# A gated decoder block: turning K on VectorE instead of TensorE in the second pass, with K times values moved ahead

## The chip, the core and the metric

The kernel runs on one core of a Trainium2 chip. The metric is the device time of one execution in microseconds (us). The kernel before took 1733.4 us, the median of 3 runs (1732.51 to 1734.95).

The engines are named as in the profile: PE (TensorE, matrix products), PEld (its weight loads), DVE (VectorE), ACT (ScalarE), POOL (GpSimd) and SP (SyncE, which only issues transfers). Each engine works off its own instructions strictly in their order and waits where an operand isn't ready.

## The reference, cut to what matters

One layer on 2048 tokens of width 1024. A normalised and modulated input is projected at once into eight parts; one branch is a pooling mixer, the other a gated linear recurrence with 8 heads of 128 channels; both are gated, merged and projected out. The change concerns the recurrence alone. Per head, with f the forget gate, k = 1 - f, and chunks of tokens:

```
o_inter = q * exp(cum) @ state
scores[t, s] = sum_k q[t, k] * k[s, k] * exp(cum[t, k] - cum[s, k])     (s <= t)
o = o_inter + scores @ v
state = exp(last) * state + (k * exp(last - cum)).T @ v
```

The last line, the update of the state, needs K with its decay to the chunk's end, multiplied by the values v with the sum over tokens. TensorE sums over partitions, so tokens have to lie on partitions there. K is made with channels on partitions: it has to be turned.

## The kernel before, in words

The 2048 tokens are done in two passes of 1024 tokens (p = 0 and 1), and each pass in two halves of 512 (t = 0 and 1, tiles of 128 channels x 512 tokens, or four blocks of 128 tokens). A pass goes through the heads 0 to 7. For each head it runs three "quads" of projections. A quad computes a 2x2 block of products by seven products named B11, T1, T2, B21, T3, B22 and T4, in this order, each of 12 matmuls of 128x512. Quad "fq" makes forget gate and query of the head, "m" the merge gates, "gp" a pooling part and the head's output gate (heads 0 to 6 run fq, m, gp; head 7 runs fq, gp, m). A quad accumulates in three PSUM banks: pa (B11, then T2, T3 and T4 on top), pe (T1, then B22) and pb. After T3, DVE adds pa into the tile c22 (L651), after B22 pe into c12 (L655). T4 accumulates into the bank pa that c22's addition reads, so it can't start before that.

Between the products the generator `hgrn` (L677) does the recurrence of the heads, one step per product. The `yield`s in it mark the steps, and both halves t step side by side. The recurrence of a head starts after its fq quad and goes on into the next head's fq and m quads. Its parts, with the names in the profile:

- F, the forget gate, is bounded from below by DVE (L681); Q (sq in the profile) is multiplied by F; a tree of products of F over 2, 4, ... 128 tokens is made in TT (L696).
- The scores are made in four sets, for token distances 1 to 4, to 8 and 16, to 32, and 64, as small matmuls into the bank psa (L756, L805 to L808), five steps apart (GAP, L800). Behind each of the first three, DVE copies the results under masks into PT (L727, L733) and multiplies K by decays one level up (`kup`, L710 to L712), and Q likewise. x32 and x64 are Q with decays for the fourth set.
- With the fourth scores issued, `kup(32)` and `kup(64)` bring K to its last level (L812, L813). These are the DVE rows K<-K,TT of 256 elements.
- Two steps later TensorE turns K by matmuls with the identity into PSUM tile pk (L819), and ScalarE copies that into KS (L821).
- Two steps later again come the products pd = KS x values (L826), four per half, and on DVE the chain SC of states, one block after the other (L831).
- Three steps later follows the output po (L839, L840), with its norm, a turn back (pot) and the gate.

In the second pass the matmuls are held in the order in which the code issues them (`line`, L346 to L353). The other engines' orders come from the framework's scheduler, which also chooses the buffers; so what stands where on DVE is read from the program's order.

Of the kernel before, what the change touches and what calls it, by code (L numbers as in the profile page):

```python
# [8 lines left out]
F32 = mybir.dt.float32  # L9
# [9 lines left out]
P = 128  # L19
SEQ = 2048  # L20
D = 1024
T = 512
NT = T // P
# [3 lines left out]
NH = 8  # L27
# [8 lines left out]
GAP = 5  # L36
# [36 lines left out]
def tile_block(ctx: ExitStack, tc: tile.TileContext, x, w_ada, b_ada, g_post, w_in, pool_w, w_pool_o, w_hgrn_o,  # L73
               w_out, ident_d, mask_d, icnt_d, w_pv_t, x_t, w_quad, w_po, rows_d, out):
    nc = tc.nc
    V, A, G, PE, SP = nc.vector, nc.scalar, nc.gpsimd, nc.tensor, nc.sync
# [14 lines left out]
    px = ctx.enter_context(tc.tile_pool(name="px", bufs=2, space=bass.MemoryType.PSUM))  # L91

    def utile(name, dt=F32):
        return up.tile([P, T], dt, tag="u", name=name)
# [4 lines left out]
    def after(ins):  # L99
        return tc.issue_after(ins.ins) if ins is not None else nullcontext()  # L100
# [245 lines left out]
    def mm(o, l, r, start, stop):  # L346
        with after(line["it"] if line["on"] else None):
            line["it"] = PE.matmul(o, lhsT=l, rhs=r, start=start, stop=stop, skip_group_check=True)  # L348
        return line["it"]

    def turn(o, i):
        with after(line["it"] if line["on"] else None):
            line["it"] = PE.transpose(o, i, ident)  # L353

    def three(ps, w, rhs, start, stop):

        hi, lo = w
        n = len(rhs)
        for k in range(n):
            wh, wl = hi[:, k * P:(k + 1) * P], lo[:, k * P:(k + 1) * P]  # L360
            rh, rl = rhs[k]
            mm(ps, wh, rh, start and k == 0, False)
            mm(ps, wh, rl, False, False)
            mm(ps, wl, rh, False, stop and k == n - 1)
# [126 lines left out]
    def v2(ap, n):  # L491
        return ap.rearrange("p (a b) -> p a b", b=n)

    def bc(ap, n):
        return ap.unsqueeze(2).broadcast_to([P, ap.shape[1], n])

    def tt(o, a, b, op=MUL, e=None):
        return (e or V).tensor_tensor(o, a, b, op=op)  # L498
# [91 lines left out]
    def h_in(p, t, k, cx):  # L590

        if (t, k) in cx["h32"]:
            src = cx["h32"][t, k]
            if t in cx["rr"]:
                tt(src, src, cx["rr"][t])
        else:
            src = px.tile([P, T], F32, tag="px", name=f"xT{p}_{t}_{k}")
            for tk in range(NT):
                xs = cx["xc"][t, k // 2][tk // 2][:, tk % 2, (k % 2) * P:(k % 2 + 1) * P]
                PE.transpose(src[:, tk * P:(tk + 1) * P], xs, ident)  # L600
            cx["h32"][t, k] = utile(f"h32_{p}_{t}_{k}")
        h32 = cx["h32"][t, k]
        A.activation(h32, src, AF.Identity, bias=shv[:, k:k + 1], scale=scv[:, k:k + 1])
        nm = ("B11", "B21", "B12", "B22")[2 * t + k % 2]
        return part(p, nm, k // 2, h32, cx)
# [19 lines left out]
    def quad(name, cx, got, tick):  # L625
# [3 lines left out]
        def prod(ps, nm, start):  # L629
            three(ps, take(), [mv[nm, i] for i in range(4)], start, True)  # L630
# [45 lines left out]

    def hgrn(p, h, t, cx):  # L677
        n = f"{p}_{h}_{t}"
        F, Q = cx["F"].pop((h, t)), cx["Q"].pop((h, t))
        A.activation(F, F, AF.Identity, bias=lb[:, h:h + 1], scale=oml[:, h:h + 1])  # L680
        V.tensor_scalar(F, F, 1e-30, None, op0=MAX)  # L681
# [2 lines left out]
        K = utile("K" + n)  # L684
# [5 lines left out]
        o = 0  # L690
        for hh in (1, 2, 4, 8, 16, 32, 64):
            w = T // (2 * hh)
            a = v2(Tb[hh], 2)
# [10 lines left out]
        def te(hh, i):  # L704
            return v2(Tb[hh], 2)[:, :, i]

        def vv(cc):
            return vh[:, t * NT + cc, :]

        def kup(hh):  # L710
            a = v2(K, 2 * hh)[:, :, 0:hh]
            tt(a, a, bc(te(hh, 1), hh))  # L712

        def qup(hh):
            a = v2(Q, 2 * hh)[:, :, hh:2 * hh]
            tt(a, a, bc(te(hh, 0), hh))
# [3 lines left out]
        def put(dst, src):  # L720

            w = src.shape[2]
            if len(dst.shape) == 3:
                m = mask[:, moff[0]:moff[0] + 4 * w].rearrange("p (a b) -> p a b", b=w)
                moff[0] += 4 * w
                shp = [P, NT, 4, w]
                V.copy_predicated(dst.rearrange("p (c a) b -> p c a b", c=NT), m.unsqueeze(1).broadcast_to(shp),  # L727
                                  src.unsqueeze(2).broadcast_to(shp))
                return
            a, b = dst.shape[2:]  # L730
            m = mask[:, moff[0]:moff[0] + NB * w].rearrange("p (c q a b) -> p c q a b", c=NT, q=4, b=b)
            moff[0] += NB * w
            V.copy_predicated(dst.rearrange("p (c q) a b -> p c q a b", c=NT), m,  # L733
                              src.rearrange("p c (a b) -> p c a b", b=b).unsqueeze(2)
                              .broadcast_to([P, NT, 4, a, b]))

        def blk(ap, b, hh):

            r = ap.rearrange("p (b a w) -> p b a w", b=b, w=2 * hh)[:, :, :, hh:2 * hh]
            return r[:, :, 0, :] if T // b == 2 * hh else r  # L740
# [12 lines left out]
        def scores(X):  # L753
            for i in range(NB):
                r0 = (i % 4) * 32
                mm(s48[r0:r0 + 32, i // 4, 0:48], K[:, i * 32:(i + 1) * 32], X[:, i, :], True, True)  # L756

        def build(hh, b, w):
            X = qp.tile([P, b, 3 * w], F32, tag="qr", name=f"X{hh}_{n}")
            A.copy(sub(X, 0, w, hh), blk(Q, b, hh))  # L760
            qup(hh)
            qo = blk(Q, b, 2 * hh)
            A.copy(sub(X, 1, w, 2 * hh), qo)
            tq = Tb[hh].rearrange("p (a b) -> p a b", b=4)
            xr = sub(X, 2, w, 2 * hh)
            tt(xr, qo, bcb(tq[:, :, 1], b, 2 * hh))
            tt(qo, xr, bcb(tq[:, :, 0], b, 2 * hh))
            return X
# [13 lines left out]
        for hh in (2, 8):  # L782
            scores(X)
            put(blk(ptf, NB, hh), s48[:, :, 0:16])
            put(blk(ptf, NB, 2 * hh), s48[:, :, 16:32])
            put(blk(ptf, NB, 2 * hh), s48[:, :, 32:48])
            kup(hh)
            kup(2 * hh)
            if hh == 2:
                X = build(8, NB, 16)  # L790
            else:
                X = qp.tile([P, T], F32, tag="qr", name=f"X32_{n}")
                x32 = X[:, 0:T // 2].rearrange("p (b w) -> p b w", w=32)
                A.copy(x32, blk(Q, NB // 2, 32))
                qup(32)
                x64 = X[:, T // 2:T].rearrange("p (b w) -> p b w", w=64)
                tq = Tb[32].rearrange("p (a b) -> p a b", b=4)
                q64 = blk(Q, NT, 64)
                tt(x64, q64, bc(tq[:, :, 1], 64))
            for _ in range(GAP):  # L800
                yield
        s64 = s48
        for cc in range(NT):
            o = cc * P
# [4 lines left out]
        A.copy(pt[0:64, :, 64:128], s64[0:64, :, 32:96])  # L809
        A.copy(pt[0:32, :, 32:64], s64[0:32, :, 0:32])  # L810
        A.copy(pt[64:96, :, 96:128], s64[64:96, :, 0:32])
        kup(32)  # L812
        kup(64)  # L813
        tt(q64, x64, bc(tq[:, :, 0], 64))
        yield
        yield
        pk = px.tile([P, T], F32, tag="px", name="pk" + n)
        for cc in range(NT):
            turn(pk[:, cc * P:(cc + 1) * P], K[:, cc * P:(cc + 1) * P])  # L819
        KS = utile("KS" + n)  # L820
        A.copy(KS, pk)  # L821
        yield
        yield
        pd = px.tile([P, NT, P], F32, tag="px", name="pd" + n)
        for cc in range(NT):
            mm(pd[:, cc, :], KS[:, cc * P:(cc + 1) * P], vv(cc), True, True)  # L826
        SC = utile("SC" + n)
# [3 lines left out]
            V.scalar_tensor_tensor(nxt, sts[-1], Tb[128][:, cc:cc + 1], pd[:, cc, :], op0=MUL, op1=ADD)  # L831
            sts.append(nxt)
        carry[h] = sts[NT]
        yield
        yield
        yield
        po = px.tile([P, NT, P], F32, tag="px", name="po" + n)
        for cc in range(NT):
            mm(po[:, cc, :], pt[:, cc, :], vv(cc), True, False)  # L839
# [221 lines left out]
    def a_job(p, j, cx):  # L1061
        w = take()
        sm = sig_in(p, j, 0, cx)
        for t in range(2):
            ps = bank(f"psA{p}_{j}_{t}")
            three(ps, w, [cx["gP"][g, t] for g in range(NG)], True, True)
            tt(sm[t], ps, sm[t])
            cx["a"][j, t] = sm[t]
            tick()
# [300 lines left out]
    for p in range(NPASS):  # L1370
# [3 lines left out]
        if p == 0:  # L1374
# [14 lines left out]
            late = [lambda k=k: h_in(0, 1, k, cxs[0]) for k in range(KT)]  # L1389
# [48 lines left out]
        for h in range(NH):  # L1438
            if 0 < h < NH - 1:
                v_head(p, h + 1, cx)  # L1440
            n = f"{p}_{h}"
# [20 lines left out]
            if h == 0:  # L1462
                for z in range(2):
                    v_head(p, z, cx)
            active.extend(hgrn(p, h, t, cx) for t in range(2))
            if wt:
                pv_merge(h // 2, wt)
# [54 lines left out]
        late = []  # L1522
# [75 lines left out]
```

## Time and profile before

| | us |
|---|---|
| runs, median (lowest to highest) | 1733.4 (1732.51 to 1734.95) |
| the profiled execution | 1732.42 |
| its span in the profile | 1730.6 |
| PE busy | 1706.8 |
| DVE busy | 1223.3 |
| ACT busy | 853.2 |

The profile is of one execution. The heads of the second pass lie at about 1000 to 1500 us. A row of a timeline has the start in us from the span's start, the duration, the engine, the source line, the operation, out<-in and the count of instructions merged; brackets hold the idle time before it and who ended it. A row of a group has, behind the bar, busy us and the mean ns of one instruction, then the idle time before. A row of a table by stage has the stretch, its length, and the busy time of PE, PEld, DVE, ACT and POOL with instruction counts, then TensorE's granted clock, the share of the DMA engines and GB/s.

### The profile page before, as it was taken

The page shows a single profiled execution, that of the slowest core. Times are in us where ns is not written, and L with a number is a line of the kernel's source. Part 1 is how long each engine was busy: PE and PEld are TensorE (multiplying, and loading weights), DVE is VectorE, ACT ScalarE, POOL GpSimd, SP SyncE. Part 2 cuts the span into 40 slices and gives each one's busy share as a digit, 9 for nine tenths or more (in the row PEclk, how much of TensorE's full clock was granted, in tenths as well). Part 3 has the DMA queues.
Part 4 walks back from the last instruction along what each step waited for, and adds up shares of the span by engine and source line. Part 5 has one row for each costly group of instructions (what it writes and reads, how often), then busy time and mean ns, then how long its engine had stood idle before and what let it go on. Part 6 is the DMA issues. An engine that isn't in the chain of part 4 may idle for free.

```text
span 1730.6 us, 31715 instructions
## 1 busy us (share of the span) xinstructions
PE 1706.8 (99%) x11805; PEld 1405.1 (81%) x11805; DVE 1223.3 (71%) x2546; ACT 853.2 (49%) x1951; POOL 96.5 (6%) x151
## 2 busy tenths in 40 slices
PE   7999999999999999999999999999999999999998
PEld 4788888888888887878888888888888888888886
DVE  4668888897988889788787254455455545776666
ACT  5746656566565665342755334344343343434243
POOL 1100000000000000100030000000000000000002
PEclk9999999999999999999999999999999999999999
DMA  9759888788789788976795765665655655565657
GB/s 331 259 185 323 287 303 287 286 300 314 268 293 329 262 289 286 350 252 223 267 313 179 249 208 179 205 202 176 214 193 173 220 180 194 184 226 168 212 197 265
DMA packets 191262, 425.33 MB, mean 246 GB/s; under 512 B 19282, under 2 KB 44546, under 8 KB 191108
## 3 DMA queue, kind: packets, MB, share of 16 engines
q1 hardware_dynamic: 181748, 406.46, 69.2%
q10 hardware_dynamic: 9360, 16.85, 2.6%
q8 instruction: 93, 1.52, 0.4%
q14 instruction: 61, 0.50, 0.1%
HBM read 267.51 MB, written 155.71 MB: 245 GB/s over the span
## 4 chain that ended last, share of the span: by engine, by line
PE 91%; DVE 4%; DMA 2%; ACT 2%; issue 1%; SPq 0%; POOL 0%; DVEq 0%; ACTq 0%; POOLq 0%
PE pafq L348 10%; PE pagp L348 10%; PE pam L348 9%; PE psA L348 5%; PE pegp L348 5%; PE pefq L348 5%; PE pem L348 5%; PE psV L348 4%; PE raB L348 4%; PE psa L348 4%; PE ray L348 3%; PE pbfq L348 3%; PE po L348 2%; PE pbgp L348 2%; PE pbm L348 2%; PE raV L348 2%
## 5 line engine op out<-in xcount | busy, mean ns | idle before, releaser
L193 DVE TENSOR_TENSOR whl<-wr,whl 128x512 fp32r<-128x512 f32 x160 | 109.4, 689 | 38.1 <-ACT whl L192 31.2
L192 ACT CAST whl<-wr 128x512 fp32r<-128x512 f32 x160 | 99.5, 625 | 69.6 <-issue 18.0
L348 PE MATMUL pam<-hT,whl 128*128 128x512 f32 x384 | 128.2, 394 | 0.6 <-ACT c12m L634 0.5
L348 PE MATMUL pagp<-hT,whl 128*128 128x512 f32 x384 | 128.1, 394 | 0.4 <-ACT c12gp L634 0.4
L348 PE MATMUL pafq<-hT,whl 128*128 128x512 f32 x384 | 126.3, 390 | 0.0
L192 ACT CAST whl<-wri 128x512 fp32r<-128x512 f32 x76 | 47.1, 622 | 118.4 <-PE psA L348 31.5
L733 DVE COPY_PREDICATED PT<-mask,psa 128x256 f32<-128x256 uint8 x160 | 86.1, 547 | 11.9 <-PE psa L348 11.9
L348 PEld LDWEIGHTS pagp<-hT,whl 128*128 128x128 f32 x384 | 72.1, 188 | 16.3 <-ACT c12gp L634 0.5
L348 PEld LDWEIGHTS pam<-hT,whl 128*128 128x128 f32 x384 | 72.1, 188 | 15.8 <-ACT c12m L634 1.1
L348 PEld LDWEIGHTS pafq<-hT,whl 128*128 128x128 f32 x384 | 72.1, 188 | 15.2 <-ACT c12fq L634 0.2
L348 PE MATMUL psA<-Ph,whl 128*128 128x512 f32 x256 | 82.5, 395 | 0.6 <-ACT Ph L179 0.6
L348 PE MATMUL psV<-whl,hB 128*128 128x512 f32 x256 | 79.6, 394 | 1.2 <-ACT hB L1330 1.1
L498 DVE TENSOR_TENSOR K<-K,TT 128x256 f32<-128x256 f32 x192 | 80.4, 423 | 0.0
L348 PE MATMUL pagp<-lT,whl 128*128 128x512 f32 x192 | 74.9, 390 | 0.0
L348 PE MATMUL pam<-lT,whl 128*128 128x512 f32 x192 | 74.8, 390 | 0.0
L348 PE MATMUL pafq<-lT,whl 128*128 128x512 f32 x192 | 74.7, 389 | 0.0
L193 DVE TENSOR_TENSOR whl<-wri,whl 128x512 fp32r<-128x512 f32 x76 | 51.8, 686 | 23.8 <-ACT whl L192 23.0
L727 DVE COPY_PREDICATED PT<-mask,psa 128x256 f32<-128x256 uint8 (+1 forms) x96 | 52.0, 542 | 21.7 <-PE psa L348 21.7
L348 PEld LDWEIGHTS psa<-X,K 128*32 128x32 f32 x2816 | 48.6, 110 | 19.8 <-issue 17.5
L861 DVE SCALAR_TENSOR_TENSOR sgg<-pot,vec,sgg 128x512 f32<-128x512 f32 x32 | 23.1, 746 | 54.5 <-PE pot L353 54.5
L681 DVE TENSOR_SCALAR F<-F 128x512 f32<-128x512 f32 x16 | 6.8, 426 | 77.5 <-ACT F L680 77.4
L348 PEld LDWEIGHTS psV<-whl,hB 128*128 128x128 f32 x256 | 47.5, 188 | 14.0 <-ACT hB L1330 1.4
(568 smaller groups left out, 4786.7 us busy)
## 6 DMA issues: line engine op xcount, KB each, us to landing
wr<-in_w_quad_dram SPq DMA_DIRECT2D x88, 256.0 KB, 4.1
whl<-scr_y SPq DMA_DIRECT2D x36, 512.0 KB, 4.7
sm<-Sd SPq DMA_DIRECT2D x64, 256.0 KB, 5.3
whl<-scr_b SPq DMA_DIRECT2D x32, 512.0 KB, 4.0
scr_y<-rfy SPq DMA_DIRECT2D x40, 256.0 KB, 2.9
x<-in_x_dram SPq DMA_DIRECT2D x32, 256.0 KB, 4.8
wa<-in_w_ada_dram SPq DMA_DIRECT2D x32, 256.0 KB, 6.0
V<-Vd SPq DMA_DIRECT2D x16, 512.0 KB, 5.1
```

Of the source, the lines that this page charges most:

```text
L192: A.copy(w[:, 0:T], raw)
L193: V.tensor_tensor(w[:, T:2 * T], raw, w[:, 0:T].bitcast(F32), op=SUB)
L348: line["it"] = PE.matmul(o, lhsT=l, rhs=r, start=start, stop=stop, skip_group_check=True)
L498: return (e or V).tensor_tensor(o, a, b, op=op)
L681: V.tensor_scalar(F, F, 1e-30, None, op0=MAX)
L727: V.copy_predicated(dst.rearrange("p (c a) b -> p c a b", c=NT), m.unsqueeze(1).broadcast_to(shp), src.unsqueeze(2).broadcast_to(shp))
L733: V.copy_predicated(dst.rearrange("p (c q) a b -> p c q a b", c=NT), m, src.rearrange("p c (a b) -> p c a b", b=b).unsqueeze(2) .broadcast ...
L861: V.scalar_tensor_tensor(og, pot, col("ng"), og, op0=MUL, op1=MUL)
```

## The change

In the heads 0 to 6 of the second pass (`by_dve`) TensorE doesn't turn K any more.

- After the third scores, DVE also makes KD: K's first three quarters (blocks of 32 tokens) of each 128 tokens with the decays of `kup(32)` and `kup(64)`. The fourth quarter needs none, and K itself stays as it is. This takes three products per half: one of 256 elements and two of 128.
- In the four steps after that, DVE turns K by 32x32 blocks into KS: `block_turn` j takes the 32 tokens j of all four blocks, and in four instructions, one for each 32 channels, writes 32 partitions of KS from 32 partitions of KD (or K, for j = 3).
- `kup(32)`, `kup(64)`, the turn into pk and ScalarE's copy into KS go.
- pd comes right behind the fourth scores in odd heads, and two steps later in even heads (`late`), where it was four steps later before. The steps behind it are padded so that po stays where it was.

The diff, cut to its core:

```
+    def block_turn(dst, src, j):
+        d, s_ = (a.rearrange("p (c n) -> p c n", n=P) for a in (dst, src))
+        for i in range(4):
+            V.transpose(d[32 * j:32 * j + 32, :, 32 * i:32 * i + 32], s_[32 * i:32 * i + 32, :, 32 * j:32 * j + 32])
...
+        by_dve, late = p > 0 and h < NH - 1, 2 * (h % 2 == 0)
...
-            for _ in range(GAP):
+                if by_dve:
+                    KD, KS = utile("KD" + n), utile("KS" + n)
+                    tt(v2(KD, 64)[:, :, 0:32], v2(K, 64)[:, :, 0:32], bc(te(32, 1), 32))
+                    for o in (0, 32):
+                        tt(v2(KD, P)[:, :, o:o + 32], v2((KD, K)[o // 32], P)[:, :, o:o + 32], bc(te(64, 1), 32))
+            for j in range(GAP):
+                if by_dve and hh == 8 and j:
+                    block_turn(KS, K if j == 4 else KD, j - 1)
                 yield
...
-        kup(32)
-        kup(64)
+        if not by_dve:
+            kup(32)
+            kup(64)
         tt(q64, x64, bc(tq[:, :, 0], 64))
-        yield
-        yield
-        pk = px.tile([P, T], F32, tag="px", name="pk" + n)
-        for cc in range(NT):
-            turn(pk[:, cc * P:(cc + 1) * P], K[:, cc * P:(cc + 1) * P])
-        KS = utile("KS" + n)
-        A.copy(KS, pk)
-        yield
-        yield
+        if by_dve:
+            for _ in range(late):
+                yield
+        else:
...
-        yield
-        yield
-        yield
+        for _ in range(7 - late if by_dve else 3):
+            yield
```

What stands in a row changes at three places. On PE, behind T4 of head 3's fq quad (pafq1_3), where the recurrence of head 2 is at work (1_2 is pass 1, head 2), stood before:

```order
L348 MATMUL pafq1_3_12864<-hT41_3_10758,whl361_12914 128x512
L348 MATMUL pafq1_3_12864<-lT41_3_10759,whl361_12914 128x512
L348 MATMUL pafq1_3_12864<-hT41_3_10758,whl361_12914 128x512
L353 MATMUL pk1_2_0_13025<-ident_87,K1_2_0_12342 128x128 x4
L353 MATMUL pk1_2_1_13032<-ident_87,K1_2_1_12349 128x128 x4
L348 MATMUL pam1_3_13053<-hB111_0_9793,whl362_12930 128x512
```

And at the same place now:

```order
L348 MATMUL pafq1_3_12930<-hT41_3_10758,whl361_12996 128x512
L348 MATMUL pafq1_3_12930<-lT41_3_10759,whl361_12996 128x512
L348 MATMUL pafq1_3_12930<-hT41_3_10758,whl361_12996 128x512
L348 MATMUL pd1_2_0_13111<-V1_2_11488,KS1_2_0_12886 128x128 x4
L348 MATMUL pd1_2_1_13121<-V1_2_11488,KS1_2_1_12916 128x128 x4
L348 MATMUL pam1_3_13145<-hB111_0_9793,whl362_13020 128x512
```

The products pd, which stood two products later, have taken the place of the turn. For odd heads, PE in head 4's fq quad between T3 and B22, in the fourth scores of head 3 (psa1_0 is the half t = 0, psa1_1 the half t = 1):

```order
L348 MATMUL psa1_0_10909<-X32_1_3_0_13596,K1_3_0_13135 32x32
L348 MATMUL psa1_0_10909<-X32_1_3_0_13596,K1_3_0_13135 32x64
L348 MATMUL pd1_3_0_13773<-V1_3_12203,KS1_3_0_13601 128x128 x4
L348 MATMUL psa1_1_10910<-X32_1_3_1_13626,K1_3_1_13142 32x32
L348 MATMUL psa1_1_10910<-sq1_3_1_13035,K1_3_1_13142 32x64
```

Before, the scores of both halves stood together there with no pd among them; now each half's pd follows its scores. On DVE, the end of the work behind head 3's third scores and the beginning of head 4, before:

```order
L498 TENSOR_TENSOR K1_3_1_13050<-K1_3_1_13050,TT1_3_1_13115 128x16x16
L727 COPY_PREDICATED PT1_135<-mask_91,psa1_1_10910 128x16x16
L681 TENSOR_SCALAR F1_4_0_13619<-F1_4_0_13619 128x512
L498 TENSOR_TENSOR c22fq1_4_13587<-pafq1_4_13555,c22fq1_4_13587 128x512
L498 TENSOR_TENSOR sq1_3_0_13022<-X32_1_3_0_13524,TT1_3_0_13107 128x4x64
L498 TENSOR_TENSOR K1_3_0_13043<-K1_3_0_13043,TT1_3_0_13107 128x8x32
```

And now (x4 are the four instructions of one `block_turn`):

```order
L503 TENSOR_TENSOR KD1_3_1_13630<-KD1_3_1_13630,TT1_3_1_13187 128x4x32
L358 STREAM_TRANSPOSE KS1_3_0_13601<-KD1_3_0_13600 32x4x32 x4
L358 STREAM_TRANSPOSE KS1_3_1_13631<-KD1_3_1_13630 32x4x32 x4
L358 STREAM_TRANSPOSE KS1_3_0_13601<-KD1_3_0_13600 32x4x32 x4
L358 STREAM_TRANSPOSE KS1_3_1_13631<-KD1_3_1_13630 32x4x32 x4
L358 STREAM_TRANSPOSE KS1_3_0_13601<-KD1_3_0_13600 32x4x32 x4
L358 STREAM_TRANSPOSE KS1_3_1_13631<-KD1_3_1_13630 32x4x32 x4
L358 STREAM_TRANSPOSE KS1_3_0_13601<-K1_3_0_13135 32x4x32 x4
L358 STREAM_TRANSPOSE KS1_3_1_13631<-K1_3_1_13142 32x4x32 x4
L687 TENSOR_SCALAR F1_4_0_13725<-F1_4_0_13725 128x512
L503 TENSOR_TENSOR c22fq1_4_13677<-pafq1_4_13645,c22fq1_4_13677 128x512
```

The 32 turns of both halves stand in one run, ahead of the next head's F and c22fq, although the code spreads them over four steps: nothing else is left to do on DVE in those steps. The lines of the kernel have moved by 5 there (L681 is now L687, and so on).

More of the change, by code (lines that the diff above doesn't have):

```diff
@@ L811, in hgrn @@
         A.copy(pt[64:96, :, 96:128], s64[64:96, :, 0:32])
-        kup(32)
-        kup(64)
+        if not by_dve:
+            kup(32)
+            kup(64)
         tt(q64, x64, bc(tq[:, :, 0], 64))
-        yield
-        yield
-        pk = px.tile([P, T], F32, tag="px", name="pk" + n)
-        for cc in range(NT):
-            turn(pk[:, cc * P:(cc + 1) * P], K[:, cc * P:(cc + 1) * P])
-        KS = utile("KS" + n)
-        A.copy(KS, pk)
-        yield
-        yield
+        if by_dve:
[3 more added lines that the diff above has]
+            yield
+            yield
+            pk = px.tile([P, T], F32, tag="px", name="pk" + n)
+            for cc in range(NT):
+                turn(pk[:, cc * P:(cc + 1) * P], K[:, cc * P:(cc + 1) * P])
+            KS = utile("KS" + n)
+            A.copy(KS, pk)
+            yield
+            yield
         pd = px.tile([P, NT, P], F32, tag="px", name="pd" + n)
@@ L833, in hgrn @@
         carry[h] = sts[NT]
-        yield
-        yield
-        yield
+        for _ in range(7 - late if by_dve else 3):
+            yield
         po = px.tile([P, NT, P], F32, tag="px", name="po" + n)
```

## The prediction

> **What bounds the kernel now.** I read the page first: its first part, for which engine is full, and its fourth, for which engine the end hangs on.
>
> ```profile
> PE 1706.8 (99%) x11805; PEld 1405.1 (81%) x11805; DVE 1223.3 (71%) x2546; ACT 853.2 (49%) x1951; POOL 96.5 (6%) x151
> PE 91%; DVE 4%; DMA 2%; ACT 2%; issue 1%; SPq 0%; POOL 0%; DVEq 0%; ACTq 0%; POOLq 0%
> ```
>
> TensorE is busy for 99% of the span and carries 91% of the chain. Then the busy time by stage, for two stretches in the heads of the second pass, where the change lies:
>
> ```profile
> 1200.00:1300.00 100.00, 100.00 (x850) 84.06 (x849) 54.39 (x145) 39.81 (x110) 4.81 (x8) 1.00 0.64 203
> 1300.00:1400.00 100.00, 100.00 (x828) 83.19 (x827) 54.28 (x129) 38.43 (x95) 2.40 (x4) 1.00 0.60 192
> ```
>
> The second number is TensorE: it never pauses. VectorE (fourth) is busy just over half the time. So here each microsecond taken off TensorE is a microsecond off the end, each one that TensorE has to wait is one on it, and VectorE work is free as long as it fits between the things TensorE waits for. The average doesn't say whether it fits; the place does.
>
> **What TensorE is spared.** TensorE's timeline from the last fq product of head 1 (pafq) on, with head 0's pk and pd (x8 and x16 are both halves of the sequence):
>
> ```profile
> 1050.92 0.39 PE L348 MATMUL pafq<-hT,whl 128*128 128x512 f32 x1
> ...
> 1053.42 0.39 PE L348 MATMUL pafq<-hT,whl 128*128 128x512 f32 x1
> 1053.65 1.03 PE L353 MATMUL pk<-ident,K 128*128 128x128 f32 x8
> 1054.44 0.48 PE L348 MATMUL pam<-hB,whl 128*128 128x512 f32 x1
> 1054.75 0.40 PE L348 MATMUL pam<-lB,whl 128*128 128x512 f32 x1
> 1054.99 0.62 PE L348 MATMUL pam<-hB,whl 128*128 128x512 f32 x2
> ...
> 1059.75 0.39 PE L348 MATMUL pem<-hT,whl 128*128 128x512 f32 x1
> 1059.98 1.95 PE L348 MATMUL pd<-V,KS 128*128 128x128 f32 x16
> 1061.68 0.48 PE L348 MATMUL pam<-hT,whl 128*128 128x512 f32 x1
> 1061.99 0.40 PE L348 MATMUL pam<-lT,whl 128*128 128x512 f32 x1
> 1062.23 0.62 PE L348 MATMUL pam<-hT,whl 128*128 128x512 f32 x2
> ```
>
> The durations overlap, so the price is taken from starts. Inside a product they lie (1053.42 - 1050.92) / 11 = 0.227 us apart. Three such steps would take 0.68 us; across pk, 1053.42 to 1054.99, they took 1.57. So pk costs TensorE 0.89 us a head, of which 0.79 until the next product starts and 0.10 more in its slow first steps. The same reckoning for pd gives 2.48 - 0.68 = 1.80 us, of which 0.10 is again slow restart.
>
> In the seven heads pk goes: 7 x 0.89 = 6.23 us. In heads 0, 2, 4 and 6 pd takes over pk's place after T4, at its old price. In heads 1, 3 and 5 it goes between the two sequence halves' fourth scores, which already pay the restart, so 3 x 0.10 = 0.30 us goes too. **Gross gain 6.5 us.** ScalarE loses the copy into KS, which is no gain: it isn't on the path. No DMA is moved, and the rows of SP and POOL stand in their old order.
>
> **What VectorE gets, and where.** For each head: six KD products, less the four products K<-K,TT after the next head's c22fq, and 32 turns of 32x4x32. The order shows all 32 in one train, behind the KD products and ahead of the next head's F and c22fq. Between them VectorE waits today; head 3 first, with the last mask copy before the gap:
>
> ```profile
> 1243.45 0.42 DVE L498 TENSOR_TENSOR K<-K,TT 128x256 f32<-128x256 f32 x1
> 1243.78 0.42 DVE L727 COPY_PREDICATED PT<-mask,psa 128x256 f32<-128x256 uint8 x1
> 1253.01 0.43 DVE L681 TENSOR_SCALAR F<-F 128x512 f32<-128x512 f32 x1 [8.80 <-ACT F L680]
> 1254.19 0.69 DVE L498 TENSOR_TENSOR c22fq<-pafq,c22fq 128x512 f32<-128x512 f32 x1 [0.75 <-PE pafq L348]
> ```
>
> And the same F of the heads after 0, 1, 2, 4, 5 and 6:
>
> ```profile
> 1045.42 0.43 DVE L681 TENSOR_SCALAR F<-F 128x512 f32<-128x512 f32 x1 [7.96 <-ACT F L680]
> 1114.64 0.43 DVE L681 TENSOR_SCALAR F<-F 128x512 f32<-128x512 f32 x1 [8.80 <-ACT F L680]
> 1183.76 0.43 DVE L681 TENSOR_SCALAR F<-F 128x512 f32<-128x512 f32 x1 [7.17 <-ACT F L680]
> 1322.14 0.43 DVE L681 TENSOR_SCALAR F<-F 128x512 f32<-128x512 f32 x1 [6.56 <-ACT F L680]
> 1391.38 0.43 DVE L681 TENSOR_SCALAR F<-F 128x512 f32<-128x512 f32 x1 [8.80 <-ACT F L680]
> 1460.51 0.43 DVE L681 TENSOR_SCALAR F<-F 128x512 f32<-128x512 f32 x1 [5.96 <-ACT F L680]
> ```
>
> The gap is 8.80 us after each odd head, and shrinks to 5.96 over the even ones. What a VectorE instruction costs, by starts and by durations:
>
> ```profile
> 1199.82 1.56 DVE L831 SCALAR_TENSOR_TENSOR SC<-SC,TT,pd 128x128 f32<-128x128 f32 x4
> ...
> 1201.90 0.28 DVE L498 TENSOR_TENSOR TT<-TT 128x128 f32<-128x128 f32 x1
> 1202.10 0.34 DVE L831 SCALAR_TENSOR_TENSOR SC<-SC,TT,pd 128x128 f32<-128x128 f32 x1
> ```
>
> ```profile
> L831 DVE SCALAR_TENSOR_TENSOR SC<-SC,TT,pd 128x128 f32<-128x128 f32 x42 | 14.5, 345 | 1.2
> L498 DVE TENSOR_TENSOR TT<-TT 128x128 f32<-128x128 f32 x12 | 3.4, 285 | 0.0
> ```
>
> With 256 elements starts lie 0.33 us apart (1243.45 to 1243.78), with 128 0.20 (1201.90 to 1202.10): neighbours overlap. KD is one of 256 and two of 128 per half: 2 x (0.33 + 0.20 + 0.20) = 1.47 us. So a train starts 1.47 us after the gap opens: in head 3 at 1253.01 - 8.80 + 1.47 = 1245.68.
>
> Of a turn the trace of before shows nothing. It has 128 elements in each of 32 partitions, as many as the TT row. Call X the time from one turn to the next. Low end: 0.20 us, if turns overlap as other instructions do. High end: 0.40 us, the step of the SC chain, each waiting for the one before: (1.56 - 0.345) / 3. Between them lies 0.285, the TT row's whole duration, for turns that neither overlap nor wait for a semaphore. I take **X = 0.31**: nearest that row, plus a little because each turn reads and writes other partitions than its neighbour.
>
> [...]
>
> **Who waits for the train.** Scores of head 3, the B22 product behind them, and the start of T4 after heads 2, 4 and 6 (after head 0 it is the 1050.92 shown above):
>
> ```profile
> 1254.08 0.22 PE L348 MATMUL psa<-X,K 128*32 128x32 f32 x1
> ...
> 1255.60 0.50 PE L348 MATMUL pefq<-hB,whl 128*128 128x512 f32 x1
> ```
>
> ```profile
> 1189.26 0.39 PE L348 MATMUL pafq<-hT,whl 128*128 128x512 f32 x1
> 1327.64 0.39 PE L348 MATMUL pafq<-hT,whl 128*128 128x512 f32 x1
> 1466.01 0.39 PE L348 MATMUL pafq<-hT,whl 128*128 128x512 f32 x1
> ```
>
> Odd heads: the first pd comes after half of the scores, at 1254.08 + 0.76 = 1254.84, and needs turn 28 (its half's last). Fits if 28 X < 1254.84 - 1245.68 = 9.16, X < 0.327. The second pd, a pd half (0.85) and 0.76 later, needs turn 32 and is looser (0.337). Heads 1 and 5 have the same distances.
>
> Even heads: pd is far off, but F and c22fq are queued behind the train, and T4 may not overwrite pafq before c22fq has read it. F and c22fq take about 0.35 + 0.69, with the signal 1.1 us. So 32 X must be under T4's start, less 1.1, less the train's start: in head 0, 1050.92 - 1.1 - 1038.93 = 10.89, X < 0.340; in head 2 10.10, 0.316; in head 4 9.49, 0.297; in head 6 8.89, 0.278.
>
> With X = 0.31: heads 0 to 3 and 5 lose nothing, head 4 waits 9.92 - 9.49 = 0.4 us, head 6 1.0. Net 6.5 - 1.4 = 5.1 us. What is late next behind c22fq (the products Q<-Q,F, the tree of decays) has gaps to be made up in before TensorE wants its result.
>
> **The rivals.** *Turns overlap* (X from 0.20 to 0.28): no wait at all, 6.5 us gained, 1726.9. For it: every other VectorE row here overlaps. Chance 0.10.
>
> *The train is too long*, and pd and T4 wait in every head. At X = 0.37 even heads lose 32 x (0.030 + 0.054 + 0.073 + 0.092) = 8.0 us, odd ones 3 x 28 x 0.043 = 3.6: 11.6 lost against 6.5, 5.1 us slower, 1738.5. It beats the gain from X = 0.346 on; at 0.40 it costs 12 us. For it: the SC chain's step, and that nothing shows what a turn costs. Against: a turn has no semaphore between most neighbours and reads no PSUM. Chance of over 3.5 us slower (X above 0.361) 0.18. [...]
>
> *Gain and waits cancel*: X from 0.328 (3 us of waits) to 0.361, or an unforeseen wait of a few us, such as TensorE's T3 behind ScalarE, where a copy into X now stands ahead of the copy into c12m. About 1733. Chance 0.19.
>
> **How the numbers follow.** The forecast (X from 0.28 to 0.327) has 0.53. The profiled execution took 1732.42 us, 1.8 more than its span, and lies 1.0 below the median of 1733.4. 1732.4 - 5.1 = 1727.3; on the median's footing 1728.3. Its own range is 1727 to 1730. About 0.2% (3.5 us) is what a measurement of this kernel can tell from no change. Faster by more: forecast and overlap, 0.63; within: 0.19; slower: 0.18. The range runs from the overlap case less scatter, 1726.2, to the long train, 1738.5, and leaves about 0.05 below and 0.12 above.
>
> **What would show it.** Right: 56 pk matmuls gone, TensorE 6.5 us less busy in the seven heads, turns 0.28 to 0.33 us apart, F starting 2 to 3 us later than today, and TensorE waiting only ahead of T4 after heads 4 and 6, for c22fq, 1 us or so. A wait ahead of pd in the odd heads, for KS, means X above 0.327. Wrong would be turns that cost 0.35 or more, or a wait that stands elsewhere than at pd or T4.

## The result and the profile after

The changed kernel took 1729.74 us (median of 20 runs, 1727.04 to 1735.38), the kernel before 1733.43 (median of 20). The ratio is 0.9982, with a 95% interval of 0.9975 to 0.9989: 3.1 us faster, between 1.9 and 4.3. That is a little under the 3.5 us that the prediction set as the least that can be told from no change, and less than the 5.1 us of its forecast. Three executions that were far slower than all others of their kernel (2303.53 and 3463.21 us of before, 3450.21 of the last kernel below) stand in no ratio.

The profiled execution of the changed kernel needs care: it took 1735.38 us and is the slowest of the 20. The first lines of its page:

```profile
span 1733.6 us, 31823 instructions
...
PE 1705.4 (98%) x11749; PEld 1400.7 (81%) x11749; DVE 1288.8 (74%) x2784; ACT 847.5 (49%) x1937; POOL 116.7 (7%) x151
...
PE 88%; DVE 5%; DMA 4%; ACT 1%; issue 1%; SPq 0%; POOL 0%; DVEq 0%; ACTq 0%; POOLq 0%
```

The 56 matmuls are gone (11805 to 11749), VectorE has 66 us more to do, and the span is nevertheless 3.0 us longer than that of before. Where it was lost is seen from two landmarks on TensorE, the first fq product of the second pass (pafq) and the first product behind the heads (psA). Before, then after:

```profile
972.62 0.39 PE L348 MATMUL pafq<-hB,whl 128*128 128x512 f32 x1
...
1517.01 0.50 PE L348 MATMUL psA<-Ph,whl 128*128 128x512 f32 x1
```

```profile
978.75 0.39 PE L348 MATMUL pafq<-hB,whl 128*128 128x512 f32 x1
...
1519.04 0.50 PE L348 MATMUL psA<-Ph,whl 128*128 128x512 f32 x1
```

The second pass began 6.1 us later, in code that the change does not touch. Windows in the first pass show TensorE pausing and a clock of 0.93 where the execution of before had 1.00:

```profile
675.00:700.00 25.00, 22.98 (x195) 17.73 (x196) 19.21 (x40) 10.03 (x22) 0.87 (x2) 0.93 0.95 336
...
750.00:775.00 25.00, 22.61 (x95) 18.07 (x95) 18.18 (x33) 10.46 (x19) 0.00 (x0) 0.93 0.78 271
```

By the trace the clock stood at 0.50 for 3.41 us from 685.93 and again from 767.85, which by itself is some 3.4 of the 6.1 us (an estimate: half of 2 x 3.41). Seven of the eight kernels below, whose first pass is the same, began the second at 971.6 to 973.6 and one at 975.8, so this is the scatter of one execution. Another 0.9 us went behind the heads: 214.6 us from the second landmark to the end against 213.6, and 213.6 to 214.5 in the kernels below; what that hangs on was not looked into. Between the landmarks, the **head stretch**, it is 1519.04 - 978.75 = 540.29 us against 1517.01 - 972.62 = 544.39: **4.10 us gained**. Everything below is measured on this stretch, and by the period of a head, from the start of one head's first pbm product to the next one's (the last one ends at the first pbgp product of head 7, whose gp quad stands at that place):

```
head           0      1      2      3      4      5      6
before       64.68  69.18  69.19  69.19  69.18  69.19  69.19
after        63.77  68.55  68.30  68.55  68.84  68.55  69.13
gain          0.91   0.63   0.89   0.64   0.34   0.64   0.06
```

The forecast was 0.89, 0.99, 0.89, 0.99, 0.46, 0.99 and -0.14. Heads 0 and 2 came out within 0.02, heads 4 and 6 within 0.2, and all three odd heads are 0.35 too low. The busy time in the two stretches that the prediction showed of before:

```profile
1200.00:1300.00 100.00, 100.00 (x843) 83.86 (x842) 63.53 (x178) 41.88 (x116) 4.81 (x8) 1.00 0.63 203
1300.00:1400.00 100.00, 99.73 (x825) 82.71 (x825) 74.23 (x203) 36.52 (x91) 2.41 (x4) 1.00 0.60 193
```

TensorE now pauses, but for 0.27 us in 200. The turns themselves, by the rows of the tile KS (least, median and greatest duration in ns), and the train behind head 1 in VectorE's timeline:

```profile
L358 DVE STREAM_TRANSPOSE KS<-KD x168: 292/302/309, 1044.9 to 1465.2; 32x128 f32<-32x128 f32 x168
L358 DVE STREAM_TRANSPOSE KS<-K x56: 304/305/309, 1052.4 to 1467.7; 32x128 f32<-32x128 f32 x56
```

```profile
1112.46 7.55 DVE L358 STREAM_TRANSPOSE KS<-KD 32x128 f32<-32x128 f32 x24
1120.03 2.56 DVE L358 STREAM_TRANSPOSE KS<-K 32x128 f32<-32x128 f32 x8
1122.61 0.43 DVE L687 TENSOR_SCALAR F<-F 128x512 f32<-128x512 f32 x1
1122.95 0.68 DVE L503 TENSOR_TENSOR c22fq<-pafq,c22fq 128x512 f32<-128x512 f32 x1
```

From the first turn to F are (1122.61 - 1112.46) / 32 = 0.317 us a turn: X was taken at 0.31. The 24 turns from KD start 7.55 / 24 = 0.315 us apart and last 0.302: none starts before the one ahead of it has ended. In the heads' stretch TensorE waits twice in all, at the two places named:

```profile
PE pafq L348 <- DVE c22fq L503: 0.8, 2, 0.5
```

```profile
1330.49 0.39 PE L348 MATMUL pefq<-hB,whl 128*128 128x512 f32 x1
1331.15 0.50 PE L348 MATMUL pafq<-hT,whl 128*128 128x512 f32 x1 [0.27 <-DVE c22fq L503]
...
1467.89 0.39 PE L348 MATMUL pefq<-hB,whl 128*128 128x512 f32 x1
1468.81 0.50 PE L348 MATMUL pafq<-hT,whl 128*128 128x512 f32 x1 [0.54 <-DVE c22fq L503]
```

Without a wait T4 starts 0.227 us behind the last pefq. It starts 1331.15 - 1330.49 - 0.23 = 0.43 us late behind head 4 and 0.69 behind head 6; the forecast was 0.43 and 1.03. After each pause the first steps are slow again, about 0.15 us more: from its first matmul to its last T4 takes 2.64 us (1331.15 to 1333.79) and 2.65 (1468.81 to 1471.46), where eleven steps of 0.227 are 2.50.

What is off is in the odd heads, where no wait stands at all. TensorE at the fourth scores of head 1, before:

```profile
1115.71 0.22 PE L348 MATMUL psa<-X,K 128*32 128x32 f32 x1
...
1117.23 0.50 PE L348 MATMUL pefq<-hB,whl 128*128 128x512 f32 x1
```

And after:

```profile
1120.95 0.22 PE L348 MATMUL psa<-X,K 128*32 128x32 f32 x1
...
1121.76 1.16 PE L348 MATMUL pd<-V,KS 128*128 128x128 f32 x8
1122.85 0.22 PE L348 MATMUL psa<-X,K 128*32 128x32 f32 x1
...
1123.67 1.16 PE L348 MATMUL pd<-V,KS 128*128 128x128 f32 x8
1124.58 0.48 PE L348 MATMUL pefq<-hB,whl 128*128 128x512 f32 x1
```

Before, both halves' scores took 1.52 us and pd, at its own place, 1.80: 3.32. Now scores and pd take 1124.58 - 1120.95 = 3.63. The prediction had 0.10 off; it is 0.31 on, by these rows.

### The profile page after: what moved, and what is told of

Same layout as the page of the kernel before. It is cut to its first block, busy times and chain, and to the rows that moved or that the text cites. A ratio compares the mean times of both kernels' runs of the same rounds, so it can differ in the third digit from the quotient of the medians.

```text
span 1733.6 us, 31823 instructions
## 1 busy us (share of the span) xinstructions
PE 1705.4 (98%) x11749; PEld 1400.7 (81%) x11749; DVE 1288.8 (74%) x2784; ACT 847.5 (49%) x1937; POOL 116.7 (7%) x151
## 4 chain that ended last, share of the span: by engine, by line
PE 88%; DVE 5%; DMA 4%; ACT 1%; issue 1%; SPq 0%; POOL 0%; DVEq 0%; ACTq 0%; POOLq 0%
PE pam L348 10%; PE pagp L348 9%; PE pafq L348 9%; PE psA L348 5%; PE pem L348 5%; PE pegp L348 5%; PE pefq L348 4%; PE ray L348 3%; PE psV L348 3%; PE psa L348 3%; PE raB L348 3%; PE po L348 3%; PE pbgp L348 2%; PE pbfq L348 2%; PE pbm L348 2%; PE raV L348 2%
## 5 line engine op out<-in xcount | busy, mean ns | idle before, releaser
L503 DVE TENSOR_TENSOR K<-K,TT 128x256 f32<-128x256 f32 x164 | 69.3, 424 | 1.2 <-PE psa L348 1.2
L865 POOL TENSOR_SCALAR ss<-ss 128x4 f32<-128x4 f32 x32 | 8.2, 257 | 865.3 <-ACT junk L864 831.0
L348 PEld LDWEIGHTS psA<-Ph,whl 128*128 128x128 f32 x256 | 48.7, 191 | 12.9 <-ACT Ph L179 2.8
```

The source lines that it names most:

```text
L865: G.tensor_scalar(ss, ss, 1.0 / P, EPS, op0=MUL, op1=ADD)
```

## The experiments

The theory after the result: the odd heads lose 0.35 us each against the forecast because pd stands between the scores of the two halves, so that TensorE goes from narrow matmuls (32 columns of weights) to full ones and back twice; and heads 4 and 6 lose 0.55 and 0.85 to the length of the train. The rivals: pd waits for the turns there in a way that the waits don't show, or the train costs TensorE something in every head.

**The turns left out.** Everything stands where it stood, but there is no train; pd takes K itself, so the state is not the reference's:

```
-                    KD, KS = utile("KD" + n), utile("KS" + n)
+                    KD, KS = utile("KD" + n), K
...
-                if by_dve and hh == 8 and j:
-                    block_turn(KS, K if j == 4 else KD, j - 1)
```

> The 32 turns of each of the seven heads are left out and pd takes K itself as its weights, so the state is not the right one; all else, KD's products and the places of pd too, is as in the changed kernel. Measured by the stretch from the first fq product of the second pass to the first product behind the heads: 544.4 us before, 540.3 after the change. Theory: in the odd heads it is not a wait for KS that takes back 0.35 us a head, but TensorE going from the scores to pd and back, twice, as pd stands between the two halves' scores; and the train of turns costs about 1.4 us in all, ahead of T4 after heads 4 and 6. Then the waits go and the odd heads stay as they are: 7 heads at 4 x 0.89 + 3 x 0.64 = 5.5 us under before, 538.9. Rival: pd waits for KS in the odd heads; then they too come to 0.99 and the stretch to 537.9.

It took 1728.01 us in one run (before, on that chip: 1732.68), and the head stretch 538.82 us. Periods of heads 0 to 6: 63.78, 68.54, 68.28, 68.54, 68.28, 68.54, 68.28. TensorE waits nowhere in the stretch. The odd heads kept 68.54 with no turn to wait for, so their loss is not a wait. Heads 4 and 6 came down to the 68.28 of head 2: the train cost them 0.56 and 0.85 and nothing elsewhere.

**The same number of turns, without a change of partitions.** Each turn reads and writes the same 32 partitions (so it turns other blocks than the kernel needs):

```
-            V.transpose(d[32 * j:32 * j + 32, :, 32 * i:32 * i + 32], s_[32 * i:32 * i + 32, :, 32 * j:32 * j + 32])
+            V.transpose(d[32 * j:32 * j + 32, :, 32 * i:32 * i + 32], s_[32 * j:32 * j + 32, :, 32 * (i % 3):32 * (i % 3) + 32])
```

> The turns read the same 32 partitions that they write, so that the four turns in a row of one block keep their partitions (the blocks that come out are the wrong ones). Theory: a turn is held until the one before has finished because its input lies in other partitions; without that turns overlap as other VectorE instructions of 128 elements do, 0.20 to 0.24 us apart in place of 0.317, the train takes 6.5 to 7.7 us in place of 10.1, and the waits ahead of T4 after heads 4 and 6 are gone: stretch 538.9. Rival: a turn takes its 0.30 us whatever its neighbours, then 0.31 apart and 540.3 as after the change.

It took 1726.55 us in one run, the head stretch 538.83, the same periods as without turns to 0.01, and no wait. VectorE's train behind head 1:

```profile
1106.05 4.98 DVE L358 STREAM_TRANSPOSE KS<-KD 32x128 f32<-32x128 f32 x24
1111.04 1.68 DVE L358 STREAM_TRANSPOSE KS<-K 32x128 f32<-32x128 f32 x8
1113.41 0.43 DVE L687 TENSOR_SCALAR F<-F 128x512 f32<-128x512 f32 x1 [0.69 <-ACT F L686]
```

Turns now start 4.98 / 24 = 0.208 us apart, as the TT products of before did (0.20), against 0.315 (7.55 / 24) when the partitions change. The train ends 0.69 us before F wants to start. So with its partitions unchanged a turn is spaced like the TT products of its size; what makes X 0.31 is that turns which change partitions did not overlap here. By this pair of runs that costs 0.107 us for each of 32 instructions.

**A longer train.** Eight turns are made twice, 40 in place of 32:

```
                     block_turn(KS, K if j == 4 else KD, j - 1)
+                    if j == 1:
+                        block_turn(KS, KD, 0)
```

> The first block turn of each half is done twice: 40 turns in a train in place of 32. Theory: VectorE's train stands right ahead of what TensorE waits for, so that past the slack each turn costs its 0.317 us. Train 12.7 us; with the slack of 10.9, 10.1, 9.5 and 8.9 us the even heads wait 1.8, 2.6, 3.2 and 3.8 us ahead of T4, and the odd ones 36 x 0.317 - 9.3 = 2.1 us each ahead of pd: 17.8 us in place of 1.4, some 16 us over the changed kernel, about 1746 us and slower than before by 0.7%. Rival: VectorE has room (55% busy), 8 turns more cost little, under 4 us.

It took 1753.59 us (median of 4), ratio 1.0131, interval 1.0110 to 1.0151: 22.7 us slower than before (0.0131 times 1733). The profiled execution is the quickest of the four, 1748.44 us; its head stretch is 560.92 us, 4.2 more than the 556.7 of the theory (538.9 and 17.8 of waits). TensorE's waits in it:

```profile
PE pafq L348 <- DVE c22fq L503: 9.4, 4, 3.2
PE pd L348 <- DVE KS L358: 6.7, 3, 2.2
```

Against the kernel without turns heads 0, 2, 4 and 6 took 1.81, 2.34, 2.97 and 3.53 us more, close to what was expected. The odd heads took 3.82, 3.80 and 3.83 more, with a wait of 2.2 as expected: each lost some 1.6 us that no wait shows. In windows of 1 us around the pd of head 1, the last number but two is the granted clock of TensorE:

```profile
1118.00:1119.00 1.00, 0.00 (x0) 0.00 (x0) 0.96 (x4) 0.00 (x0) 0.00 (x0) 1.00 0.87 344
1119.00:1120.00 1.00, 0.79 (x4) 0.82 (x5) 0.94 (x4) 0.00 (x0) 0.00 (x0) 0.58 0.00 0
1120.00:1121.00 1.00, 1.00 (x6) 0.96 (x5) 0.95 (x4) 0.00 (x0) 0.00 (x0) 0.50 0.11 25
1121.00:1122.00 1.00, 1.00 (x27) 0.81 (x28) 0.75 (x2) 0.55 (x2) 0.00 (x0) 0.50 0.00 0
1122.00:1123.00 1.00, 1.00 (x17) 0.83 (x15) 0.89 (x2) 0.98 (x5) 0.00 (x0) 0.72 0.00 0
```

After the pause the clock stands at 0.50 from about 1119.16 to 1122.56, 3.4 us (worked out from the means 0.58 and 0.72 of the windows at the ends), and head 1's first pd and the second scores take 1.98 and 1.42 us to the next group's start (1119.21, 1121.19, 1122.61), against 1.09 and 0.82 in the changed kernel. So the price of a train that is too long, which the prediction reckoned as waits alone, is in the odd heads of this execution nearly double that. The other three executions have lower mean clocks (0.994, 0.992 and 0.994 against 0.996), which suggests that more such stretches made them slower; no trace of them is kept. When a pause lowers the clock is taken up in the last section.

**pd in the odd heads one step later**, behind both halves' scores and the product B22:

```
-        by_dve, late = p > 0 and h < NH - 1, 2 * (h % 2 == 0)
+        by_dve, late = p > 0 and h < NH - 1, 1 + (h % 2 == 0)
```

> late is 1 in place of 0 in the odd heads: pd comes one product later, behind B22, by itself. Theory: it no longer breaks up the scores and costs its 1.80 us as before, so the odd heads gain 0.89 us like the even ones instead of 0.64: stretch 539.5, 0.8 us under the changed kernel. Rival: sharing the fourth scores' place saves a restart of TensorE (0.10 us a head, as the prediction had it), so that moving pd away loses: 540.6.

It took 1727.74 us (median of 6), ratio 0.9973, interval 0.9961 to 0.9984. The head stretch is 539.37, the odd heads 68.26 each, 0.29 less than in the changed kernel and 0.93 less than before. The even heads are as in the changed kernel (68.82 and 69.10 for heads 4 and 6).

**pd directly behind both halves' scores.** In the odd heads the state step is put on a list and run at the end of the step, when both halves have issued their fourth scores:

```
+        if by_dve and late == 0:
+            put_off.append(state_step)
+        else:
+            state_step()
...
+        while put_off:
+            put_off.pop(0)()
```

> In the odd heads both halves' pd come behind both halves' scores, in the same step, instead of each behind its own half's. Theory: the two extra changes between scores and pd go, and the restart behind them is shared, so the odd heads gain 0.89 to 0.99 us instead of 0.64: stretch 539.2 to 539.5. Rival: the changes between small and large matmuls cost nothing, pd's place among the scores does not matter: 540.3.

It took 1729.23 us in one run (before, on that chip: 1733.82), the head stretch 539.39, the odd heads 68.26, 68.25 and 68.25. TensorE in head 1:

```profile
1115.78 0.22 PE L348 MATMUL psa<-X,K 128*32 128x32 f32 x1
...
1117.30 2.05 PE L348 MATMUL pd<-V,KS 128*128 128x128 f32 x16
1119.11 0.48 PE L348 MATMUL pefq<-hB,whl 128*128 128x512 f32 x1
```

Scores 1.52 and pd 1.81, as at two separate places before (1.52 and 1.80). So the restart is not shared even here: the change from scores to pd costs as much as one from scores to a product. The rows also show where the changed kernel loses. There the two groups of scores take 0.81 and 0.82 (1120.95 to 1121.76, 1122.85 to 1123.67), 0.11 more than 1.52, and the two pieces of pd 1.09 and 0.91, 0.19 more than 1.81. Together that is 0.30 us a head, the 0.29 of the periods.

**pd back at its old place**, four steps after the fourth scores, in all seven heads:

```
-        by_dve, late = p > 0 and h < NH - 1, 2 * (h % 2 == 0)
+        by_dve, late = p > 0 and h < NH - 1, 4
```

> late is 4 in all seven heads: pd stays at the step where it was before the change, only the turning moves to VectorE. Theory: moving pd ahead has no worth of its own, what gains is the seven turns on TensorE that go: 7 x 0.89 less the same 1.4 us ahead of T4: stretch 539.6. Rival: the new place is part of the gain, and the stretch goes back over 540.3.

It took 1727.74 us in one run, the head stretch 539.37, the odd heads 68.26 each. Three places for pd, one stretch: 539.37, 539.39, 539.37. Moving pd earlier earned nothing anywhere; it only cost where it came between the halves.

**The train shortened ahead of c22fq.** In the even heads the last eight turns, those of K itself, are issued behind the next head's c22fq:

```
+        last["c22"] = tt(s5, a, s5, op=ADD)
...
-                if by_dve and hh == 8 and j:
+                if by_dve and hh == 8 and j and (j < 4 or h % 2):
...
+            if h % 2 == 0:
+                with after(last["c22"]):
+                    block_turn(KS, K, 3)
```

> In the even heads the last of the four block turns (K's own, 4 turns a half) comes behind the next head's c22fq, since pd is two products off; odd heads as in the changed kernel. Theory: the waits ahead of T4 after heads 4 and 6 (0.55 and 0.83 us by the trace) go, as c22fq then comes 2.5 us sooner: stretch 538.9. Rival: T4 waits for something else, or the eight turns behind c22fq delay c12fq instead: 540.3 or more.

It took 1728.02 us in one run, the head stretch 539.56: the theory's 538.9 was missed by 0.7. Head 4 fell to 68.32, but head 6 only from 69.13 to 68.96. The waits of TensorE in the stretch, and VectorE behind head 6:

```profile
PE pagp L348 <- ACT pbgp L644: 0.4, 1, 0.4
```

```profile
1451.67 7.55 DVE L358 STREAM_TRANSPOSE KS<-KD 32x128 f32<-32x128 f32 x24
1459.26 0.43 DVE L687 TENSOR_SCALAR F<-F 128x512 f32<-128x512 f32 x1
1459.60 0.68 DVE L503 TENSOR_TENSOR c22fq<-pafq,c22fq 128x512 f32<-128x512 f32 x1
...
1464.49 0.69 DVE L503 TENSOR_TENSOR c12fq<-pefq,c12fq 128x512 f32<-128x512 f32 x1
```

Both waits ahead of T4 are gone. In their place stands one in the gp quad of head 7, for ScalarE's copy of pagp into pbgp: the product behind it starts at 1472.33 where 1471.59 + 0.23 was due, 0.51 us late, and the slow first steps come on top, 0.69 in all for head 6. That copy, in the changed kernel and in this one:

```profile
1477.47 0.59 ACT L644 COPY pbgp<-pagp 128x512 f32<-128x512 f32 x1
```

```profile
1471.70 0.58 ACT L644 COPY pbgp<-pagp 128x512 f32<-128x512 f32 x1
```

Counted from the start of the head stretch (978.75 and 973.05) it starts at 498.7 us in both. The eight turns have only moved behind c22fq, among the steps that lead to c12fq, so what ScalarE does behind c12fq is no earlier than it was; only TensorE is, and it waits there instead. The other traces agree. Counted in the same way, the addition into c12fq starts at 491.53 in the changed kernel and at 491.44 here, and the copy follows 7.2 us later in both. Without turns the addition starts at 488.96 and the copy at 496.65, and no wait stands there. In the kernel with pd at its old place ScalarE works in another order, and the copy follows by 4.8 us. So the copy is late by the train ahead of c12fq and by ScalarE's order; no run changed that order alone.

**Both: pd behind the scores, and the train split in even heads** (the two edits above together):

> Both mends together: pd of the odd heads behind both halves' scores, and the last block turn of the even heads behind the next c22fq. Theory: nothing is left of the waits and of the breaks, so the gross gain stands: 7 x 0.89 to 6.5 us, stretch 537.9 to 538.2, 1727 to 1728 us, 0.3% faster than before. Rival: something else is late next, and it stays at the changed kernel's 1729.7.

Its median was 1729.32 us (of 9) against 1733.82 of before on that chip, ratio 0.9970, interval 0.9960 to 0.9981. The head stretch is 538.67, the shortest of all the kernels that compute the reference: 5.72 us under before. The periods are 63.78, 68.25, 68.27, 68.26, 68.33, 68.25 and 68.94; head 6 keeps its 0.7 and the wait for pbgp (0.36 us), so the 537.9 to 538.2 was not reached. By the stretch it is 1.62 us better than the changed kernel; the intervals of the ratios (0.9975 to 0.9989, and 0.9960 to 0.9981) overlap, so the times alone don't show it.

## Why the prediction was right, and where not

Its way was right: TensorE was the bound, what was taken off it came off the time, and VectorE's work was free except where the train met T4. Of the outcomes that it weighed, 3.1 us by the ratio lies just under the 3.5 us with which its forecast began, and 3.7 by the medians just over; that the change itself is worth more than 3.5 us is shown by the stretch (4.10), not by the times. Step by step:

- **The price of pk, 0.89 us a head: right.** Heads 0 and 2 gained 0.91 and 0.89, and without any turns the even heads gained 0.90, 0.91, 0.90 and 0.91.
- **The odd heads' 3 x 0.10 for a shared restart: wrong, and the step that failed.** It took the scores' restart as one that pd could use too. Measured, the odd heads gained 0.64 and not 0.99, 1.05 us less in all. The runs split this in two. pd directly behind both scores gained 0.93, and pd at its old place, away from the scores, gained 0.93 too, so nothing is shared. And pd between the halves costs 0.29 more, twice from narrow matmuls to full ones and back: both the scores (0.11) and pd (0.19) pay for a second start. The order that the change section shows had the scores, pd, scores, pd in plain sight; the prediction counted the restarts of products and not those of the scores and pd themselves.
- **X = 0.31: right** (0.317 measured), an estimate from the 0.285 of the TT row, and for the reason given: with the partitions unchanged it is 0.208. Rivals that needed other values of X, overlap and a train that is too long, did not come about.
- **The waits: right in place and near in size.** None in heads 0 to 3 and 5, then 0.56 and 0.85 in heads 4 and 6, 1.41 us in all where 1.4 was forecast (1.46 by its own bounds). That the total fits so well is luck, as two errors cancel in the parts: head 6's wait itself was 0.69 and not 1.03, and the slow steps after each pause, 0.15, were left out.
- **The sum.** 5.1 less 1.05 is 4.05; the stretch gave 4.10. The times gave 3.1, with 4.1 inside the interval. TensorE is 4.9 us less busy in the stretch (544.39 to 539.48) and not 6.5, mostly for the odd heads' sake.
- **The long train's price, 12 us at X = 0.40: too low.** Its own bounds give 17.9 - 6.5 = 11.4 there. With 40 turns, as long as 32 at 0.40, the stretch came out 16.5 us over that of before in the profiled execution. Without the 1.6 us that the halved clock, which the sum didn't know, added in each odd head, it would be 11.7: the waits were as reckoned.

The rival that an unforeseen wait of ScalarE takes the gain did not come about in the changed kernel, but its like, the pbgp copy, turned up as soon as the wait ahead of T4 was removed behind head 6.

What stays open: whether another order on ScalarE would win the 0.7 us of head 6 in the last kernel, and whether the 1.6 us between it and the changed kernel hold over many executions.

## What to carry to other kernels

When a matmul group is moved, count the changes of form on TensorE along the whole new order, also those between the pieces that it now parts (0.30 us a head here); a place beside other small matmuls was not a cheaper place (a stretch of 539.39 us against 539.37 at the old one). A train of turns that hop between groups of 32 partitions took full durations here (0.315 us a turn), not the overlapped spacing of its neighbours (0.20), and what mattered of it was the first instruction of the next stage queued behind it (c22fq, 0.56 and 0.85 us in heads 4 and 6). When a wait has been removed, look up which engine is next late before counting the whole of it as gain (head 6 kept 0.69 us of its 0.85).

## What the hardware showed unexpectedly

**Pauses and the clock.** In the run with the longer train, a pause of 2.24 us behind the narrow scores of an odd head took the clock to 0.50, and a longer pause of 3.24 us behind full-width products, in head 6, did not lower it. The two places in TensorE's timeline, with the idle time in brackets, and the clock in the second:

```profile
1119.21 2.05 PE L348 MATMUL pd<-V,KS 128*128 128x128 f32 x8 [2.24 <-DVE KS L358]
...
1482.80 0.50 PE L348 MATMUL pafq<-hT,whl 128*128 128x512 f32 x1 [3.24 <-DVE c22fq L503]
```

```profile
1481.00:1482.00 1.00, 0.00 (x0) 0.00 (x0) 0.96 (x4) 0.00 (x0) 0.00 (x0) 1.00 0.89 328
1482.00:1483.00 1.00, 0.20 (x1) 0.20 (x2) 0.97 (x4) 0.22 (x1) 0.00 (x0) 1.00 0.18 70
```

So the length of a pause alone doesn't decide.

What the traces show: the low stretches last 3.41 us each, or more at a kernel's end (5.21 in the changed kernel), and within a trace their starts lie whole multiples of 3.413 us apart: in the changed kernel's first pass 685.93 and 767.85 (81.92 us, 24 times 3.413), here 1119.15 and 1262.51 (42 times; as far again, at 1405.87, TensorE is in pd of head 5, which lasts 1.96 us as against 1.16 in the changed kernel). So time can be cut into windows of 3.413 us on that grid, and TensorE's idle time summed in each:

| window | TensorE idle in it, us | clock right behind it |
|---|---|---|
| long train, heads 1, 3: ends at 1119.15, 1262.51 | 2.18, 2.23 | 0.50 |
| long train, head 5: ends at 1405.87 | 2.24 | below 1.00, by pd's 1.96 us |
| long train, head 6: ends at 1480.96, 1484.38 | 1.40, 1.84 | 1.00 |
| long train, heads 0, 2, 4: the fuller window of each | 1.18, 1.25, 1.65 | 1.00 in head 4; in heads 0 and 2 T4 takes 2.62 us from its first matmul to its last, no longer than in head 4 |
| changed kernel, first pass: ends at 685.93, 767.85 | 1.99, 2.09 | 0.50 |
| before, behind the heads: ends at 1725.78 | 1.80 | 1.00 |

The pause of 3.24 us lay across the end of a window, 1.40 us in one and 1.84 in the next; those of 2.24 lay almost wholly in one. Narrow scores are not needed for it: the window that ends at 767.85 has full-width products alone. In the traces of before and of the changed kernel, from 16 us on, the clock fell behind every window with 1.99 us of idle time or more and behind none with 1.80 or less; in the long train's heads it fell behind 2.18 and more and not behind 1.84 (the ends of matmuls are modelled, so the boundary is no sharper than that). So in these traces a pause of some 2 us in one window cost the half clock, and one of 3.24 across two did not; that all three odd heads were hit is chance as far as these runs show.

**A turn on VectorE.** 32 partitions x 128 elements of f32 last 0.302 and 0.305 us (from KD and from K) when the partitions change. When they don't, the row of the larger group reads:

```profile
L358 DVE STREAM_TRANSPOSE KS<-KD x168: 256/258/304, 1038.5 to 1455.6; 32x128 f32<-32x128 f32 x168
```

That is 0.258 us by the median, with starts 0.208 us apart.

**The same first pass** took from 971.6 to 978.8 us in the ten profiled executions shown or told of here. One profile's span can hide a change of this size; a stretch between two landmarks did not (the periods of a head in different kernels agreed within 0.06 us where its code was the same).
